# From alternating token tiles to two contiguous token ranges, feature-major, with a list scheduler: a transformer block on eight cores

## The chip, the cores and the metric

One Trainium2 chip, all 8 of its cores. Four pairs of cores take one batch element each. The metric is the device time of the slowest core, in microseconds. A program on all cores has a second, slower state in some executions: the cores of one die show a lower granted clock (0.81 to 0.96 on average where an undisturbed die has 0.96 to 0.98) and the time is 2 to 16% longer.

Engines: PE is TensorE's matmul side and PEld its weight loads, DVE is VectorE, ACT ScalarE, POOL GpSimd, SP the engine that issues the plain DMA queue. GpSimd issues the queue that casts fp32 weights to bf16 on the way.

## The reference

```python
# x: (4, 2048, 2048) fp32; one layer
hn = rms_norm(h, g_pre_mix);  z = hn @ w_in          # [u | q | k | v | f_logit]
y_pool = multiscale_pool(u, w_pool, pool_scale)       # trailing means over 2, 4, 8, 16 frames
y_attn = forgetting_attention(q, k, v, log_sigmoid(f_logit + b_f))   # 8 heads of 128, causal
y = concat(rms_norm(y_pool), rms_norm(y_attn))
h = h + rms_norm(y @ w_out, g_post_mix)
m = square(relu(rms_norm(h, g_pre_mlp) @ w_up)) @ w_down              # 2048 -> 8192 -> 2048
h = h + rms_norm(m, g_post_mlp)
gate = sigmoid(rms_norm(h, g_ple_gate) @ w_gate)
h = h + rms_norm(gate * (p @ w_ple), g_post_ple)
```

## The kernel before

Each core of a pair owns every second tile of 128 tokens (1024 tokens), and all eight run one program. K and V are made for all 2048 tokens on both cores. After the attention the data lie token by feature, so the features that the next matmul contracts over must be brought onto the partitions by transposes on TensorE. Instructions are issued in the order in which Python records them; two streams are interleaved with generators.

```python
def attention(hp, ...):             # the denominator is a 129th column of V
    va = VA[sn][:, tt, hh, 0:129]
    mm(bank(b, 0, 129), pt[:, 0:128], va, first, ...)
    ...
def out_part(i, q):                 # token tile i, 512 output features
    for kc in range(KC):
        mm(bank(b), yT[:, i, kc, :], wout[q][:, kc, :], kc == 0, kc == KC - 1)
    actf(junk(), bank(b), AF.Square, accum=col1(ssq_o, i * 4 + q))   # a sum of squares per row
...
def norm1(i):                       # the statistic is a column: no matmul
    v_sum(col1(s_o, i), ssq_o[:, i * 4:i * 4 + 4])
    rsqrt(col1(r_o, i), col1(s_o, i), float(D))
    v_stt(o, o, col1(r_o, i), xt[i % 2], ALU.mult, ALU.add)
    ...
def transpose_tile(src, gi, dst):   # 16 PE transposes for 128 tokens, then gains on the way out
    pe.op(lambda h: h.transpose(tv[:, k, :], src[:, kc * 128:kc * 128 + 128], ident), ...)
...
def gate(w, q, t):
    ...
    actf(sg, bank(b), AF.Sigmoid, scale=col1(r_3, t))
```

Row sums of squares come out of ScalarE as a by-product (`accum`), and normalising is one VectorE instruction per tile with a per-partition scalar. Hardly anything is asked of GpSimd but DMA issue and 16 copies.

The softmax here doesn't subtract the row's maximum and nothing guards it: scores larger than these inputs give would overflow.

## Time and profile before

| | before |
|---|---|
| time, median of 5 runs | 1696.18 us (1695.76 to 1698.33) |
| TensorE busy | 1590.8 us, 94% |
| VectorE, ScalarE, GpSimd busy | 558.5, 505.1, 121.3 us |
| mean granted clock | 0.98 |
| TensorE work at the prediction's price per matmul | 1560 us |
| the rest: idle and slow-clock time | 136 us |

Every matmul that the trace records is given the prediction's price for its columns; the sum over a core's matmuls, subtracted from the elapsed time of a stage, leaves what the stage lost. The lines of the profile of before that carry the price are in the prediction. (An fp32 matmul is recorded as two, each at the price of a bf16 one. That is too little: at full clock such a record took 203 ns for 240 columns, twice the price. So in the changed kernel some 8 us of "loss" are work, the same 8 in every run below.)

### The profile page before, as it was taken

The page shows a single profiled execution, that of the slowest core. Times are in us where ns is not written, and L with a number is a line of the kernel's source. Part 1 is how long each engine was busy: PE and PEld are TensorE (multiplying, and loading weights), DVE is VectorE, ACT ScalarE, POOL GpSimd, SP SyncE. Part 2 cuts the span into 40 slices and gives each one's busy share as a digit, 9 for nine tenths or more (in the row PEclk, how much of TensorE's full clock was granted, in tenths as well). Part 3 has the DMA queues.
Part 4 walks back from the last instruction along what each step waited for, and adds up shares of the span by engine and source line. Part 5 has one row for each costly group of instructions (what it writes and reads, how often), then busy time and mean ns, then how long its engine had stood idle before and what let it go on. Part 6 is the DMA issues. An engine that isn't in the chain of part 4 may idle for free.

```text
span 1696.4 us, 24256 instructions; the slowest of 8 cores (1691.1 to 1696.4 us)
## 1 busy us (share of the span) xinstructions
PE 1590.8 (94%) x8700; PEld 812.8 (48%) x8700; DVE 558.5 (33%) x915; ACT 505.1 (30%) x1071; POOL 121.3 (7%) x241
## 2 busy tenths in 40 slices
PE   3789999999968999999999999999999999998995
PEld 1447585855544444444444444444444444444442
DVE  3564232322535553112111211121221112475455
ACT  3564544445432543110001100011000111445355
POOL 2012000001000001000101010100101010001000
PEclk9999999999988999999999999999999999999998
DMA  9566223138173549644444353526353546557736
GB/s 241 136 159 93 34 30 46 27 50 125 20 155 50 158 143 190 106 66 84 74 77 78 72 87 63 99 51 100 53 97 62 88 69 134 160 185 188 148 125 223
DMA packets 42308, 175.71 MB, mean 104 GB/s; under 512 B 4688, under 2 KB 4944, under 8 KB 33616
## 3 DMA queue, kind: packets, MB, share of 16 engines
q0 software_dynamic: 31824, 103.20, 37.9%
q1 hardware_dynamic: 10368, 70.96, 12.5%
q8 instruction: 73, 1.20, 0.3%
q14 instruction: 43, 0.35, 0.1%
HBM read 252.16 MB, written 25.17 MB: 163 GB/s over the span
## 4 chain that ended last, share of the span: by engine, by line
PE 84%; DVE 4%; ACT 4%; DMA 4%; issue 3%; DVEq 0%; ACTq 0%; POOL 0%; POOLq 0%; SPq 0%
PE pb L306 83%; DMA wring<-wqkv 1%; DMA grow<-gb 1%; DVE m L339 1%; DVE accd L334 1%; PE pb L687 1%; DVE m L334 1%; ACT sq L324 1%; ACT junkb L324 1%; DMA wring<-wv 1%; ACT h1j L324 1%; DMA pT_sb<-pT 0%; ACT stats L324 0%; ACT VA L324 0%; ACT rstdB L324 0%
## 5 line engine op out<-in xcount | busy, mean ns | idle before, releaser
L306 PE MATMUL pb<-hT,wslot 128*128 128x512 bf16 x2048 | 442.8, 379 | 2.0 <-DVE hT L334 2.0
L306 PE MATMUL pb<-wslot,hidden 128*128 128x512 bf16 x2048 | 443.7, 379 | 0.0
L306 PEld LDWEIGHTS pb<-hT,wslot 128*128 128x128 bf16 x2048 | 200.3, 98 | 243.3 <-issue 2.1
L306 PEld LDWEIGHTS pb<-wslot,hidden 128*128 128x128 bf16 x2048 | 200.1, 98 | 240.3
L324 ACT ACTIVATE rt<-pb 128x512 f32<-128x512 f32 x128 | 76.4, 598 | 691.1 <-PE pb L306 690.6
L334 DVE TENSOR_TENSOR hidden<-rt 128x512 bf16<-128x512 f32 x128 | 88.5, 692 | 352.0 <-ACT rt L324 352.0
L324 ACT ACTIVATE ptb<-pb,biasT 128x256 bf16<-128x256 f32 (+1 forms) x320 | 139.5, 454 | 163.7 <-PE pb L306 162.4
L334 DVE TENSOR_TENSOR m<-m,pb 128x512 f32<-128x512 f32 x96 | 64.8, 686 | 206.5 <-PE pb L306 206.5
L67 POOL DMA_DIRECT2D wslot<-wmlp x128 | 67.9, 548 | 870.1 <-PE pb L306 833.1
L306 PE MATMUL pb<-wslot,hT 128*128 128x512 bf16 x512 | 119.1, 387 | 0.9 <-ACT sgt L324 0.9
L306 PE MATMUL pb<-wo,yT 128*128 128x512 bf16 x512 | 116.7, 385 | 0.0
L306 PE MATMUL pb<-hgo,wring 128*128 128x512 bf16 x384 | 102.9, 389 | 11.9 <-DMA wring<-wqkv 11.9
L306 PE MATMUL pb<-wring,hgo 128*128 128x256 bf16 (+1 forms) x512 | 69.4, 282 | 21.4 <-DMA wring<-wv 15.2
L306 PE MATMUL pb<-VA,ptb 128*128 128x129 bf16 x576 | 82.6, 220 | 4.0 <-ACT ptb L324 3.0
L306 PEld LDWEIGHTS pb<-wslot,hT 128*128 128x128 bf16 x512 | 50.8, 100 | 63.5 <-issue 5.8
L306 PE MATMUL pb<-wring,hgp 128*128 128x256 bf16 (+1 forms) x512 | 70.4, 276 | 11.6 <-DVE hgp L329 11.6
L306 PE MATMUL pb<-QT,KT 128*128 128x256 bf16 (+1 forms) x320 | 79.6, 262 | 0.0
L306 PEld LDWEIGHTS pb<-wo,yT 128*128 128x128 bf16 x512 | 49.9, 99 | 56.6 <-issue 1.7
L306 PEld LDWEIGHTS pb<-VA,ptb 128*128 128x128 bf16 x576 | 53.5, 98 | 34.8 <-issue 9.5
L306 PEld LDWEIGHTS pb<-wring,hgo 128*128 128x128 bf16 x512 | 49.9, 100 | 38.8 <-issue 28.6
L306 PE MATMUL pb<-wu,hgo 128*128 128x512 bf16 x256 | 65.9, 383 | 0.0
L324 ACT ACTIVATE junkb<-m 128x512 bf16<-128x512 f32 x64 | 40.3, 630 | 75.5 <-DVE m L334 74.2
(112 smaller groups left out, 1163.3 us busy)
## 6 DMA issues: line engine op xcount, KB each, us to landing
wslot<-wmlp POOLq DMA_DIRECT2D x128, 512.0 KB, 12.0
xst<-xT SPq DMA_DIRECT2D x16, 1024.0 KB, 6.7
wring<-wqkv POOLq DMA_DIRECT2D x36, 256.0 KB, 8.5
wo<-wout POOLq DMA_DIRECT2D x16, 512.0 KB, 15.3
xt<-xo SPq DMA_DIRECT2D x8, 1024.0 KB, 6.8
h1s<-osb SPq DMA_DIRECT2D x8, 1024.0 KB, 9.1
h1t<-h1s SPq DMA_DIRECT2D x8, 1024.0 KB, 6.7
wslot<-wgate POOLq DMA_DIRECT2D x16, 512.0 KB, 27.5
```

Source lines behind the costliest of these rows:

```text
L67: self.h.dma_start(out=out, in_=in_).then_inc(s[0], 16)
L306: pe.op(lambda h: h.matmul(o, lhsT, rhs, start=bool(start), stop=bool(stop), skip_group_check=True), r=(lhsT, rhs), w=(o,), signal=bool(st ...
L324: act.op(lambda h: h.activation(o, i, func, **kw), r=r, w=w)
L334: (eng or dve).op(lambda h: h.tensor_tensor(o, a, b, op), r=(a, b), w=(o,))
L339: dve.op(lambda h: h.scalar_tensor_tensor(o, a, s, b, op0, op1, accum_out=accum), r=r, w=w)
L687: pe.op(lambda h, k=k, kc=kc: h.transpose(tv[:, k, :], src[:, kc * 128:kc * 128 + 128], ident), r=(src[:, kc * 128:kc * 128 + 128], ident) ...
```

## The change

The intent: fewer columns for TensorE (K and V only where they are needed, no transposes), no waiting between token tiles, and every engine's order decided by a scheduler instead of by hand. Even cores run one program ("arm a") for tokens 0 to 1087, odd cores another ("arm b") for tokens 1088 to 2047, which still needs K and V of all tokens, its own range and the "context" before it. Everything stays feature by token. So a norm's sum over features is a sum over partitions: squares are added up over the 16 feature blocks into one accumulator tile, on VectorE and on GpSimd, and a matmul with a matrix of ones (tile `onesm`) sums and spreads it. The diff replaces nearly the whole file; its core:

```diff
+    def schedule(self, ops):          # list scheduler: earliest start first, then order of recording
+        ...
+                    key = (st, o.idx)
+                    if pick is None or key < pick[0]:
+                        pick = (key, o)
+        ...
+                else:
+                    t = o.end + 0.2   # a result is there 0.2 us after its assumed end
...
-    def transpose_tile(src, gi, dst, r=mmr):
...
-        actf(sg, bank(b), AF.Sigmoid, scale=col1(r_3, t))
+        P.act(s, (pv, 0, w), AF.Exp, scale=-1.0)
+        P.act(s, s, AF.Ln, bias=1.0)
+        P.act(s, s, AF.Exp, scale=-1.0)
...
+    def sumsq(src, acc_, w, firstone, eng, pool=sqo):
+        ...
+            P.act(t[:, 0:w], src, AF.Square)
+            P.tt(acc_[:, 0:w], acc_[:, 0:w], t[:, 0:w], add, eng=eng)
...
+    def out_norm(g):
+        ...
+            P.tt(O4, O4, rBo[:, 0:w].unsqueeze(1).to_broadcast([128, 4, w]), mult)
+            P.tt(O4, O4, X[:, :, 0:w], add, eng="pool" if q == 1 else "dve")
+        ...
+            for k in range(4 * q, 4 * q + 4):
+                sumsq(O[:, k, 0:w], A2, w, k == 0, "pool" if k % 2 else "dve", sqn)
+        ...
+        P.pe([P.mm(pt, onesm, A2[:, 0:w], 0, w, True, True)])
...
+    P.dma("gq", wps, io["wpool"])
...
+    for g in (0, 1):
+        for blk in range(16):
+            down_last(g, blk)          # last quarter of the down projection, token group g
+        scale2(g)
+        norm2(g)                       # recorded ahead of group g + 1
...
+    with nc.If((pid % 2) < 1):
+        arm(True)
+    with nc.Else():
+        arm(False)
```

The accumulators are `aco` (output norms), `n` (norm before the gate) and `acz` (last norm); `m` is the residual in SBUF that the down projection and the gate are evicted into; `st` holds pieces of h1 or h2 read back from HBM; `xs` holds arriving x. A suffix `_a` or `_b` names the arm.

## The prediction

> **What bounds the kernel now.** I read the page's busy table, then the clock and DMA rows of the 40 slices, the chain that ended last, the windows cut at the stage borders, and the instruction groups.
>
> ```profile
> PE 1590.8 (94%) x8700; PEld 812.8 (48%) x8700; DVE 558.5 (33%) x915; ACT 505.1 (30%) x1071; POOL 121.3 (7%) x241
> PE   3789999999968999999999999999999999998995
> ...
> PEclk9999999999988999999999999999999999999998
> DMA  9566223138173549644444353526353546557736
> ...
> PE 84%; DVE 4%; ACT 4%; DMA 4%; issue 3%; DVEq 0%; ACTq 0%; POOL 0%; POOLq 0%; SPq 0%
> ```
>
> TensorE is the bound (84% of the chain), with three weak places: the first three slices, slices 11 to 15, and the last few. The windows and the chain in order of time size them:
>
> ```profile
> 0.00:130.00 130.00, 85.12 (x460) 47.29 (x461) 67.21 (x155) 65.75 (x87) 14.62 (x32) 0.95 0.73 177
> ...
> 400.00:520.00 120.00, 104.04 (x722) 61.27 (x720) 48.69 (x89) 53.85 (x155) 5.02 (x10) 0.91 0.51 95
> 520.00:659.00 139.00, 127.57 (x716) 64.34 (x716) 72.68 (x85) 57.51 (x112) 7.67 (x15) 0.98 0.56 143
> ...
> 1457.00:1550.00 93.00, 83.43 (x466) 40.15 (x463) 62.41 (x57) 48.69 (x95) 7.39 (x14) 1.00 0.59 180
> ...
> 1674.00:1696.40 22.40, 4.31 (x20) 1.76 (x18) 9.73 (x15) 8.11 (x15) 0.00 (x0) 0.67 0.51 189
> ```
> ```profile
> 222.65 86.02 PE pb L306 x671
> ...
> 659.37 797.89 PE pb L306 x3696
> ```
>
> (Window columns: span, busy us and count of PE, weight load, DVE, ACT, POOL, then clock, DMA share, GB/s.) From 659.4 to 1457.3 nothing but TensorE is on the chain: 797.89/3696 = 215.9 ns per 512-column matmul, i.e. columns/2.4 ns plus 2.6 ns. The 86.02 us piece has 671 narrower ones over 200,848 columns: (86,020 - 83,690)/671 = 3.5 ns over. So I price a matmul at columns/2.4 plus 2.6 ns (3.3 ns below 400 columns). Counting the old code's matmuls that way gives, in us, K 111, V 113, Q 55, U 62, attention 65, output projection 111, PE transposes 22, pooling 12, MLP 885, gate 111, PLE 14, statistics 3: **1561**. The other 135 us of 1696 are idle or slow-clock time: startup 129.6 us for 73 us of priced work (56 lost), some 40 around 400-659, some 39 after 1457.
>
> **What the Trainium skill says.**
> - "TensorE: Matmul & The Clock Gate", Part 1: a back-to-back warm matmul costs N/2.4 plus about 2.5 ns. The 215.9 ns agrees.
> - The same part warns of a 13/16 clock once three cores of a die run dense matmuls. This trace doesn't show it: eight cores ran the MLP at 1.00. I take the clock as unchanged.
> - "ScalarE: Activation LUTs", Table sets: a change of function set costs a load of about 2.7 us, and one set holds both exp and ln. The trace has 17 loads of 1.283 us, half the figure; two of these sit in the tail. The change replaces Sigmoid by Exp, Ln, Exp, so nearly all should go.
> - "SBUF — State Buffer", Who interferes with whom: a VectorE instruction with two SBUF inputs and a GpSimd instruction that reads SBUF lock each other out. The old kernel cannot test it: its only GpSimd arithmetic is 16 copies. The new one gives GpSimd hundreds of adds.
>
> ```profile
> L334 DVE TENSOR_TENSOR m<-m,pb 128x512 f32<-128x512 f32 x96 | 64.8, 686 | 206.5 <-PE pb L306 206.5
> L334 DVE TENSOR_TENSOR accd<-accd,sq 128x512 f32<-128x512 f32 x56 | 38.7, 692 | 12.4 <-ACT sq L324 8.1 <-DVE accd L334 1.0
> ...
> L334 DVE TENSOR_TENSOR m<-m,h1t 128x2048 f32<-128x2048 f32 x8 | 18.3, 2293 | 1.4 <-DVE m L339 1.4
> ...
> L324 ACT ACT_TABLE_LOAD x17 | 21.8, 1283 | 9.7 <-DMA xst<-xT 8.4 <-DVE stats L348 0.9
> ```
>
> VectorE on fp32 pairs: (2293 - 692)/1536 = 1.042 ns per column plus 158 ns. ScalarE, from 598 ns at 512 and 1054 at 1024 columns: 0.89 ns per column plus 142.
>
> **The change part by part.** It is a rewrite. Before, each core of a pair takes every second 128-token tile, and all eight run one program with K and V for 2048 tokens. Now an even core runs an arm for tokens 0-1087, with K and V for those alone; an odd core runs an arm for 1088-2047, with K and V for all 2048. Everything stays feature-by-token, so no PE transposes; norm sums become matmuls with a matrix of ones; the attention denominator moves from a 129th V column to a VectorE sum; a list scheduler written into the kernel orders every engine's instructions.
>
> *1. TensorE work, priced as above.* Even arm (us): K, Q, V 182, attention 43, U 59, pooling 7, output 119, up 475, down 475, gate 119, PLE 15, fp32 statistics (four passes per column, as I count them) 15: **1510**. Odd arm: 275, 90, 53, 7, 106, 417, 417, 106, 13, 15: **1498**. Against 1561: saves 51 on the longer arm. The two are within 12 us, so the uneven split 1088/960 looks deliberate.
>
> *2. Startup.* Now 16 chunks of x (8.9 MB), with K and most of Q multiplied as chunks arrive; four weight blocks of 0.52 MB (as bf16) first. Rates from the queue table: the plain queue moved 70.96 MB in 12.5% of 1696 us, 335 GB/s when busy; the casting queue 103.2 MB in 37.9%, 160 GB/s. So 8.9/335 + 2.1/160 = 26.6 + 13.1 = 40 us, plus some 2 us latency and 5 us of statistics, by which V's weights have come: 47 us. TensorE has 22 us of work in it. VectorE per chunk: a scale in two of three (about 0.7 us) and an add of 1088 (1.29), 1.8 us by 16 = 28 us, hidden. Lost: 47 - 22 and some 3 of low clock = **28**, against 56. The old startup, after its first 38 us, was held by square-and-add chains between slabs, not by DMA.
>
> *3. Last attention with pooling.* VectorE, odd arm: 82 denominator adds over 24,448 columns 38.4, masks 4, closings 8; pooling per channel block: evacuation 1.33, window adds 1.75 times 1.17, difference 1.16, scaling 1.32, by 8 = 47. Sum 97 us against 82 of TensorE: 15 lost, plus GpSimd collisions, say **18**. Even arm: 82 against 77: **8**.
>
> *4. Head norms and output projection.* The norm chain (two matmuls, four ScalarE steps, first scaling) about **5**. Output groups: VectorE 23 and GpSimd 9 us per 30 us of TensorE, tight: **4**. The MLP starts on the first two thirds of the tokens, covering the last norm. These replace the old 40 around 400-659.
>
> *5. MLP.* Same bytes per column as before (1.05 MB read per 7.3 us); nothing lost.
>
> *6. From the last down projection.* Norms are hidden per token group behind the next group's matmuls. VectorE adds up to about 190 us of 226, GpSimd 80-100, and many pairs exclude each other: **8**, up to 30 if the lock is strict.
>
> *7. Tail.* The last group has 176 tokens: activations 1.5, sum and statistic 2, 16 scalings at 0.34 and some five adds at 0.52: 8; store 2: **13**, against 18 from the last matmul before.
>
> *8. Branch on the core's number*: **3**, a guess.
>
> Even: 1510 + 28 + 8 + 5 + 4 + 8 + 13 + 3 = 1579. Odd: 1498 + 28 + 18 + 5 + 4 + 8 + 13 + 3 = 1577. Predicted: **1580 us**, 6.8% less. Of the 116 us gain some 51 is less TensorE work, 28 the startup, the rest the middle and the end.
>
> **The rivals.**
> - *VectorE and GpSimd become the bound outside the MLP.* For: steps 3 and 6 are near full before any collision, and a static order can't absorb a late operand. Against: idle VectorE now (33%), and the scheduler was given these durations (its 0.157 + 1.042 per thousand columns is the trace's). It would add 20-50: 1600-1630.
> - *The scheduler fills nearly everything.* For: tens of matmul groups are free to move while one waits. Then only startup, tail and a few gaps remain: 1510 + 40 = 1550.
> - *Transfers.* Pieces of 1.0-1.2 KB per row replace 8 KB rows for x, h1, h2 and the result, and weight loads queue behind GpSimd adds; output weights land where the activations lay, so they wait for the last U matmul. Against: a DMA share of 0.5 now in the MLP. Would add 10-40.
> - *One arm is longer.* The time is the slowest core's; a miscount of one arm goes straight into it, and a gain on the other is worth nothing.
>
> **Range and chances.** The first three rivals span 1550 to 1630; an eight-in-ten range is 1545 to 1628. To miss 2% (1662), losses would have to be 150 us, more than the old kernel's, despite its much worse startup: at or above that I give 8%. Faster by over 2% 0.92, within 0.06, slower 0.02.
>
> **What would show it.** Right: even and odd cores within 20 us of each other, with about 10,900 and 10,100 matmuls; MLP at full clock with no waits; TensorE dense from about 47 us; one or two table loads; no transposes. Wrong: TensorE waiting in the pooling or gate stage on VectorE tiles whose mean time is well above 158 + 1.042 per column (the lock); startup beyond 60 us (DMA slower when two queues share); a gap at the first output block (weights); the two kinds of core 30 us apart; or a clock of 0.8 in the denser stages.

## The result

The changed kernel took **1711.03 us** (median of 7 timed runs, one of them slow; fast ones 1709.49 to 1713.09), against 1695.86 for the kernel before in the same rounds: a ratio of **1.0087** (95% interval 1.0076 to 1.0098). It is 0.9% slower, where 1580 was predicted. (A ratio is the mean time of one kernel's fast runs over the mean of the other's fast runs of the same rounds, so not quite the ratio of the medians quoted.) Executions in which one die ran at a lower clock are left out of the means.

The page of the changed kernel, core 3, an odd one, in the rows that the prediction shows of before (busy time, TensorE and clock and DMA in 40 slices, shares of the chain that ended last):

```profile
PE 1544.3 (90%) x10180; PEld 980.5 (57%) x10180; DVE 786.4 (46%) x1569; ACT 579.2 (34%) x1349; POOL 296.2 (17%) x392
PE   2889999999888887899999999999999999883994
...
PEclk9989999999999998899999999999999999986997
DMA  7951211236009347944544454445444443795056
...
PE 78%; DMA 7%; DVE 7%; issue 4%; ACT 2%; POOL 1%; SPq 1%; DVEq 0%; ACTq 0%; POOLq 0%
```

TensorE's busy time fell by 46 us, VectorE's rose by 228, and the chain runs through DMA and VectorE for 14% where it was 8%. The MLP, slices 18 to 34, is full. The weak places are the first three slices, slices 11 to 17 and, new, slices 35 to 37, after the MLP.

What TensorE waited for (columns: total us, times, longest), core 3:

```profile
PE pb L363 <- DVE m_b L420: 25.4, 3, 12.6
PE pb L363 <- DMA wsl_b<-wk: 19.7, 1, 19.7
PE pb L363 <- DVE n_b L420: 19.2, 3, 16.7
PE pb L363 <- POOL aco_b L420: 18.6, 3, 6.8
```

and core 0, an even one:

```profile
PE pb L363 <- POOL aco_a L420: 39.3, 4, 18.8
PE pb L363 <- DVE n_a L420: 18.0, 3, 11.3
PE pb L363 <- DVE m_a L420: 14.7, 3, 10.5
PE pb L363 <- DMA wsl_a<-wk: 12.5, 1, 12.5
```

Most of these are not waits for data that a large matmul needs. `aco` and `n` are accumulators that feed one small statistics matmul. TensorE takes its instructions in order; where the scheduler put that small matmul a few us before its operand was there, the large ones behind it stood as well. One such place in the timeline (start, us, engine, operation, and in brackets the idle time before):

```profile
559.74 12.77 PE L363 MATMUL pb<-yT_b,wo_b 128*128 128x240 bf16 x123
578.41 1.14 PE L363 MATMUL pb<-aco_b,onesm_b 128*128 128x240 f32 x2 [5.89 <-POOL aco_b L420]
579.34 10.88 PE L363 MATMUL pb<-yT_b,wo_b 128*128 128x240 bf16 x94
```

The output matmuls before and after the gap have nothing to do with `aco_b`, but 5.9 us are gone.

**Where the time went.** My sum over the trace, with the prediction's price for each matmul (us; "before the output" is startup, projections, attention, pooling and head norms up to the first output matmul; the output stage ends with the last statistics matmul of the output norms; "end" runs from the first matmul of the last down projection to the last gate matmul):

| | priced work | before the output | output stage | MLP | end | tail | total |
|---|---|---|---|---|---|---|---|
| odd (core 3), predicted loss | 1498 | 54 | 4 | 0 | 8 | 13 | 1577 |
| odd, found | 1492 | 97.7 | 40.0 | -1 | 61.8 | 21.1 | 1711 |
| even (core 0), predicted loss | 1510 | 44 | 4 | 0 | 8 | 13 | 1579 |
| even, found | 1503 | 77.6 | 48.5 | -2 | 52.6 | 21.3 | 1701 |

("Before the output" is the prediction's startup, pooling, head norms and branch together.) The other cores of a kind lost about the same: in this profile the four odd ones 94.9 to 97.7 us before the output and 61.7 to 62.7 in the end, the four even ones 74.7 to 77.6 and 44.3 to 52.6. In the later runs the spread is up to 10 us (the odd cores' end with the norms mixed in, 26.6 to 35.1), so smaller differences between two runs mean little unless all four cores show them.

The change took 68 us of work from TensorE (1560 to 1492; some 60 with fp32 at its measured cost) and lost 84 us more while TensorE waited or ran below full clock (136 to 220). The question is where those losses come from. Four places: startup (about 69 us in the odd arm by 416 us, 49 in the even arm by 250 us, together with the branch, 31 predicted), the pooling stage with the head norms (some 28.5 in both arms; 23 and 13 predicted), the output stage, and the end.

### The profile page after: what moved, and what is told of

Read it like the earlier page. It is cut to its first block, busy times and chain, and to the rows that moved or that the text cites. A ratio compares the mean times of both kernels' runs of the same rounds, so it can differ in the third digit from the quotient of the medians.

```text
span 1711.5 us, 29071 instructions; the slowest of 8 cores (1688.7 to 1711.5 us)
## 1 busy us (share of the span) xinstructions
PE 1544.3 (90%) x10180; PEld 980.5 (57%) x10180; DVE 786.4 (46%) x1569; ACT 579.2 (34%) x1349; POOL 296.2 (17%) x392
## 3 DMA queue, kind: packets, MB, share of 16 engines
q0 software_dynamic: 28208, 102.77, 35.1%
## 4 chain that ended last, share of the span: by engine, by line
PE 78%; DMA 7%; DVE 7%; issue 4%; ACT 2%; POOL 1%; SPq 1%; DVEq 0%; ACTq 0%; POOLq 0%
PE pb L363 78%; DMA xs_b<-xin 4%; DVE m_b L426 2%; DMA st_b<-h1s 1%; DMA xr_b<-xin 1%; DVE dac_b L420 1%; DVE m_b L420 1%; DVE acc_b L420 1%; DVE aco_b L420 1%; POOL aco_b L420 1%; DVE osb_b L420 1%; SPq L441 0%; ACT ptb_b L393 0%; POOL acz_b L420 0%; ACT sg_b L393 0%
## 5 line engine op out<-in xcount | busy, mean ns | idle before, releaser
L363 PE MATMUL pb<-hT_b,ws_b 128*128 128x480 bf16 (+3 forms) x2560 | 420.0, 327 | 10.5 <-ACT hT_b L393 10.5
L363 PEld LDWEIGHTS pb<-hT_b,ws_b 128*128 128x128 bf16 x2560 | 243.5, 98 | 185.9 <-issue 15.0
L363 PE MATMUL pb<-hid_b,ws_b 128*128 128x480 bf16 x1536 | 311.5, 366 | 0.0
L363 PEld LDWEIGHTS pb<-hid_b,ws_b 128*128 128x128 bf16 x1536 | 150.3, 98 | 160.7
L363 PE MATMUL pb<-hgo_b,wsl_b 128*128 128x512 bf16 (+2 forms) x768 | 188.9, 386 | 37.8 <-DMA wsl_b<-wk 19.7
L393 ACT ACTIVATE ptb_b<-pb,bias_b 128x256 bf16<-128x256 f32 (+3 forms) x328 | 157.8, 508 | 103.9 <-PE pb L363 60.4
L420 DVE TENSOR_TENSOR dac_b<-dac_b,ptb_b 128x256 f32<-128x256 f32 (+3 forms) x304 | 153.4, 508 | 54.8 <-ACT ptb_b L393 43.7
L363 PE MATMUL pb<-hidg_b,ws_b 128*128 128x272 bf16 (+2 forms) x1024 | 109.8, 271 | 15.2 <-DVE m_b L420 15.2
L363 PE MATMUL pb<-h2g_b,ws_b 128*128 128x272 bf16 (+2 forms) x1024 | 116.7, 270 | 3.6 <-ACT sg_b L393 3.0
L363 PE MATMUL pb<-yT_b,wo_b 128*128 128x240 bf16 x1024 | 111.2, 273 | 0.0
L363 PE MATMUL pb<-QT_b,KT_b 128*128 128x256 bf16 (+3 forms) x328 | 82.3, 290 | 1.0 <-ACT ptb_b L393 1.0
```

What stands on the lines that cost most here:

```text
L363: ins = h.matmul(pb[0:rows, pt.bank, lo:hi], lhsT, rhs, start=st, stop=sp_, skip_group_check=True)
L393: return self.rec("act", lambda h: h.activation(of(), if_(), func, **kw), r, [self.key(o)], (0.18 + 0.84e-3 * self.size(i)))
L420: return self.rec(eng, lambda h: h.tensor_tensor(of(), af(), bf(), op), [self.key(a), self.key(b)], [self.key(o)], self.vdur(o, a, b, eng))
```

## The experiments

All edits are to the changed kernel. The theories: **A**, the scheduler plans small statistics matmuls at a moment that the chain of small instructions before them can't keep, and the in-order TensorE stands there; **B**, VectorE and GpSimd lock each other out, so VectorE is late; **C**, transfers are late (x, h1 and h2 in small pieces beside the weights). Losses are given as odd / even, in the table's terms, from cores 3 and 0. All runs gave correct results unless it is said otherwise.

### A: tell the scheduler that statistics come later

```diff
-                    t = o.end + 0.2
+                    t = o.end + 0.2 + q.lag     # 6.0 for the statistics matmuls below, else 0
...
-        P.pe([P.mm(pt, onesm, A2[:, 0:w], 0, w, True, True)])
+        P.pe([P.mm(pt, onesm, A2[:, 0:w], 0, w, True, True)]).lag = LAG   # out_norm; the same in rsq
```

> Edit: only the scheduler's belief changes: the statistics matmuls of the norms (a matrix of ones times a sum of squares) are planned 6 us later than their operand's planned end. Theory A (TensorE's queue is in order, and the plan puts these matmuls before their operand is there; TensorE waits 20 us on the output norm's and some 30 us on the later norms' statistics in the odd arm, 42 and 30 in the even arm): these waits fall by more than half, odd cores 1670 to 1685 us, even cores 1650 to 1670. Theory B (VectorE and GpSimd as a pair are too slow in these stages, whatever the order): TensorE waits as long, only at other matmuls; within 10 us of 1711.

Measured: 1690.0 us (one fast run; before 1695.2 to 1697.1), mean spans 25 us less on the odd cores and 36 us less on the even ones. Output stage 40.0 / 48.5 to **20.4 / 10.2**; end 61.8 / 52.6 to 58.9 / 49.6. (The odd cores stayed just above the 1670 to 1685 expected.) No work was removed: every engine runs the same instructions as before. Their order is planned anew, though, on TensorE and, less intended, on the others too. In the output stage, 530 to 720 us, TensorE's waits in the kernel with the lag are

```profile
PE pb L365 <- ACT hT_b L395: 9.7, 2, 6.0
PE pb L365 <- DMA ws_b<-wup: 1.3, 1, 1.3
PE pb L365 <- DVE aco_b L422: 1.3, 1, 1.3
```

The wait on `aco_b`, 18.6 us, is down to 1.8 (0.5 of it for an addition on GpSimd, not shown). So theory A holds for the output stage. What the plan had wrong, the 0.2 us between engines or the durations that it assumes, this run does not separate: 6 us cover both. In the end the waits for `n_b` vanished too, but those for `m_b` grew from 25.4 to 42.2 us: there something else is late.

### B: no arithmetic on GpSimd

```diff
     def tt(self, o, a, b, op, eng="dve"):
+        eng = "dve"
```

> Edit: every GpSimd tensor addition goes to VectorE; the plan is made again. Theory B (lock between a VectorE instruction with two SBUF inputs and a GpSimd addition, and sums that pass from one engine to the other): VectorE's scalings of m drop from 719 ns to about 441 (158 + 1.042 x 272), the broadcast multiply of 960 columns from 1661 to 1158; the output and end stages lose 20 to 50 us less, the pooling stage 10 to 20 us more; in all 1670 to 1705. If the lock costs nothing: VectorE durations stay, VectorE has some 95 us more to do, 1730 to 1760.

Measured: 1704.9 us (one fast run). Output stage 49.0 / 52.3, no better; end **39.3 / 32.6**, 20 us better. The 10 to 20 us more that were expected of the pooling stage were not there: with the head norms it lost some 6 and 2 us more. Groups with two SBUF inputs on VectorE, changed kernel (busy us, then the mean in ns, ahead of the last bar), with the GpSimd adds among them:

```profile
L420 DVE TENSOR_TENSOR osb_b<-osb_b,rBo_b 128x960 f32<-128x960 f32 x16 | 26.2, 1661 | 4.0 <-ACT rBo_b L393 4.0
L420 POOL TENSOR_TENSOR aco_b<-aco_b,sqn_b 128x240 f32<-128x240 f32 x32 | 31.6, 988 | 30.9 <-DVE aco_b L420 22.5 <-ACT sqn_b L393 5.2 <-ACT sqo_b L393 2.4
L426 DVE SCALAR_TENSOR_TENSOR m_b<-m_b,cst_b,n_b 128x272 f32<-128x272 f32 x32 | 21.5, 719 | 0.2 <-ACT n_b L393 0.2
```

and the same work without GpSimd:

```profile
L421 DVE TENSOR_TENSOR osb_b<-osb_b,rBo_b 128x960 f32<-128x960 f32 x16 | 18.1, 1153 | 3.7 <-ACT rBo_b L393 3.7
L421 DVE TENSOR_TENSOR aco_b<-aco_b,sqn_b 128x240 f32<-128x240 f32 x60 | 24.3, 405 | 2.0 <-ACT sqn_b L393 1.2 <-DVE aco_b L421 0.5 <-ACT rt_b L393 0.2
L427 DVE SCALAR_TENSOR_TENSOR m_b<-m_b,cst_b,n_b 128x272 f32<-128x272 f32 x32 | 15.1, 496 | 0.3 <-ACT n_b L393 0.3
```

The same instructions take 1153 ns and not 1661, 496 and not 719. The first of the shorter figures is at the prediction's 158 ns + 1.042 ns per column (1158), the second, which also multiplies by a gain, 55 ns over it (441). The lock is real, and the longer means hide how it works. Of the sixteen 960-column multiplications in the changed kernel twelve took 1144 to 1159 ns, and four 3182 to 3193. Each of the four began while a GpSimd addition was running, here the first of them (start, us):

```profile
559.34 2.95 POOL L420 TENSOR_TENSOR osb_b<-osb_b,xr_b 128x960 f32<-128x960 f32 x1 [14.08 <-DVE osb_b L420]
560.11 3.19 DVE L420 TENSOR_TENSOR osb_b<-osb_b,rBo_b 128x960 f32<-128x960 f32 x1
```

The addition ends at 562.29, VectorE's instruction at 563.30, so it waited out the addition and did the rest, 1.01 us, after it. Evictions that take one operand from PSUM were not held up: `m_b<-m_b,pb` of 272 columns took 430 ns on the mean beside GpSimd and 434 alone.

Yet in the output stage TensorE still waits for `aco_b`, now made by VectorE alone, 31.5 us: removing the lock is no cure there, and run A, which kept GpSimd's adds, shows that the order is.

### C: first MLP weights and gate weights after the reads that they meet

```diff
-    bload(blocks[len(phys) - 1])
+    bload(blocks[len(phys) - 1], after=[xr_op[0]])     # after the last read of x
...
-        bload(("gt", 0, blk))
+        bload(("gt", 0, blk), after=[st_op[0]])        # after the second group's last read of h1
```

> Edit: the MLP's first weight blocks (all but two) are issued only after the last load of x for the output norm, and the gate's weights only after the last load of h1 of the second token group. Theory C (small loads stand behind a flood of weights: 18.5 us for x at 667, 19.1 us for h1 at 1483 in the odd arm): both long waits fall under 6 us, odd cores 1685 to 1700. Theory A or B: the waits become waits for weights or for VectorE, within 8 us of 1711.

Measured: 1717.6 and 1714.6 us, ratio to before 1.0116 (1.0087 to 1.0146), so no gain. Output stage 48.4 / 48.4, end 54.3 / 61.0. The edit did what it was meant to: the last two pieces of x landed in 6.1 and 7.2 us at most (odd, even), where they had taken 19.0 and 26.6. But the waits for `aco` did not shrink (38.0 and 39.3 us). As the bound of the output stage, theory C falls. For the end this run only shows that holding the gate weights back gains nothing; a later run shows why.

### The branch: test for odd cores first

```diff
-    with nc.If((pid % 2) < 1):
-        arm(True)
-    with nc.Else():
-        arm(False)
+    with nc.If(((pid + 1) % 2) < 1):
+        arm(False)
+    with nc.Else():
+        arm(True)
```

> Edit: the branch tests for odd cores first, so that the odd arm's code comes first and the even arm is the far side of the branch. Theory D (the far side starts 6 us later: first x load at 9.6 us in the odd arm, 3.3 in the even one): the starts change places, odd cores 1703 to 1707 us, even cores 1703 to 1708; the time 1703 to 1708. If transfers hide the late start: odd cores stay at 1709 to 1711.

Measured: 1712.0 and 1708.9 us. The odd cores are 8 us sooner (mean span 1710.4 to 1702.3), the even ones 7 us later (1696.7 to 1704.2). So the far side of the branch costs some 7 us; in the changed kernel the odd arm's first load of x is issued at 9.6 us and the even arm's at 3.3. Turning it moves the cost to the other arm.

### A and B together, first try

The lag as above, and the GpSimd adds after the MLP's last down projection (not those before the MLP) on VectorE:

```diff
-        sumsq(md, acm[g], w, blk == 0, "pool" if blk % 2 else "dve", sqm)
+        sumsq(md, acm[g], w, blk == 0, "dve", sqm)      # the same at the four other places of the end
```

> Both changes at once: the scheduler is told that the statistics matmuls of the output and later norms come 6 us later, and the GpSimd adds after the MLP's last down projection (not those before the MLP) go to VectorE. The lag alone freed the output stage (odd arm's loss 40 to 20 us, even arm's 48 to 10) and left the end at 59 and 50; the end with every add on VectorE and no lag lost 39 and 33. Theory (two independent causes, an order planned too tight in the output stage and the lock in the end): odd output loss near 20 and end loss near 39 or below, time near 1670, even cores near 1640. Rival (the end is held by VectorE's sheer work, the lock only a part of it): the lag and the moved adds overlap, end loss stays above 50 in the odd arm, time stays at 1685-1690.

Measured: 1683.45 us, ratio 0.9908 (0.9851 to 0.9965). Output stage 18.7 / 12.1, but the end 57.0 / 54.8: the 20 us that the lockless end had won were not there. The first theory, of two causes that simply add, failed here. What differs from the run without GpSimd is the lag on the statistics *after* the MLP. New theory: that lag itself costs the end as much as the lock, since there the next matmuls hang on the norm.

### The lag on the output norms alone

```diff
-        P.pe([P.mm(pt, onesm, acc_[:, 0:w], 0, w, True, True)]).lag = LAG      # rsq
+        P.pe([P.mm(pt, onesm, acc_[:, 0:w], 0, w, True, True)])
```

> As the run with the lag and the moved adds, but the lag is on the statistics matmul of the output norms alone, not on those after the MLP. Theory (the lag itself cost the end what the moved adds had won: it put the later norms 6 us later): output loss near 19 (odd) and 12 (even), end loss near 39 (odd) and 33 (even) as in the run with all adds on VectorE; odd cores near 1665. Rival (the moved adds did not free the end; the gain seen there belonged to the whole order of that kernel): end loss stays above 50.

Measured: 1671.9 and 1668.3 us, ratio 0.9829 (0.9806 to 0.9853). Output 19.5 / 9.8, end **38.6 / 38.3** (39 and 33 expected). As the new theory had it: the lag helps where other matmuls are free to move up, and costs where they are not. What remains in the end (from 1340 us on) is one kind of wait:

```profile
PE pb L365 <- DVE m_b L422: 31.0, 6, 16.0
PE pb L365 <- DVE acz_b L422: 2.9, 1, 2.9
```

`m_b` is written both by a norm and by the eviction of the next group's down projection. The scheduler prefers what was recorded first, and a whole norm (some 40 VectorE instructions) was recorded ahead of the next group. So evictions, which free TensorE's accumulators, queue behind it. That is theory D.

### D: norms mixed into the next group, GpSimd kept and not

```diff
+def mix(*parts):                       # interleave by count of instructions
+    ...
-        scale2(g)
-        norm2(g)
+    norm2(0); N = P.take()
+    for blk in range(16):
+        down_last(1, blk)
+    scale2(1); T = P.take()
+    L.extend(mix((N, 0, 0.8), (T, 0, 1)))       # the same for groups 2, 3 and for the gates
```

With GpSimd's adds kept in the end:

> Lag on the output norms as in the last run; GpSimd keeps its adds; and after the MLP each norm's instructions are recorded mixed, by count, among the next group's matmuls and their evictions, where the change records them as a block ahead. The scheduler prefers what was recorded first, so VectorE did some 40 instructions of a norm before the evictions that free TensorE's accumulators. Theory D (TensorE stands in the end because its evictions queue behind a norm on VectorE): end loss from 62 and 53 to 35 or less. Rival (the lock's longer VectorE times are the cause): end loss stays above 50, since VectorE's work and the lock are as before.

With them on VectorE:

> Both: the mixed order and the adds of the end on VectorE, with the lag on the output norms. If order and lock are independent causes, the end loss falls below both of the last two runs, to about 15-25; if they are one cause seen twice (VectorE late, whatever for), it is close to the lower of the two. Output loss 19 and 12. Odd cores 1640-1665.

Measured: 1672.0 us in both runs with GpSimd's adds, 1659.4 and 1659.9 without (ratios 0.9841 and 0.9768, the latter 0.9747 to 0.9789). The loss of the end, odd / even, all with the lag on the output norms alone except the first, which is the changed kernel itself:

| | norm ahead of the next group | norm mixed in |
|---|---|---|
| GpSimd adds in the end | 61.8 / 52.6 | 43.4 / 41.9 |
| VectorE alone in the end | 38.6 / 38.3 | 32.0 / 28.5 |

Neither expectation was met as written (35 or less against above 50; 15 to 25 against the lower of the two). Either cure gives 11 to 23 us, both give 24 to 30 (on the mean of the four cores of a kind, the cells are 62 / 49 and 42 / 42, 40 / 39 and 32 / 29, so 8 to 22 and 20 to 30). I read them as two ways for VectorE to be late for the same evictions, which is why they add only in part.

### Startup: the bytes

The pooling weights have no buffer to wait for, so they are loaded amid x, and in the even arm the first output and MLP weights wait for them and follow:

```diff
-    P.dma("gq", wps, io["wpool"])
+    P.dma("gq", wps, io["wpool"], after=[xdma[-1]])
```

> The pooling weights, and with them the first output weights that wait for them, are loaded after the last load of x and not in the middle of it. Theory (the startup is bound by the bytes that the DMA engines must move before the last chunk of x has come): 1.0 to 1.5 MB of cast weights leave the first 50 us of the even arm; at 160 GB/s of the casting queue that is some 6 us of DMA time shared with x, so the loss up to 80 us falls from 44 to about 38 in the even arm; in the odd arm 0.5 MB leave and the loss up to 130 us falls from 64 to about 61. Rival (the startup is bound by latency of each chunk's chain, load, scale, matmul): no change of more than 1 us. The time itself: 1705 to 1711.

Measured: 1710.5 and 1708.0 us. The loss up to 80 us in the even arm 43.6 to **37.7**, up to 130 us in the odd arm 64.2 to **58.8**; mean spans 8 us less (even) and 6 us less (odd).

The other test leaves out the second range of x, in the odd arm alone:

```diff
-        xdma.append(P.dma("sp", X, io["xin"][kc, :, a:b], after=after))
+        if first or b > 1024:           # the context keeps what the buffers hold
+            xdma.append(P.dma("sp", X, io["xin"][kc, :, a:b], after=after))
```

> Wrong result on purpose: the odd arm does not load x for its context range (8.4 MB) but works on what its staging buffers hold; the even arm is as it was. Theory (the odd arm's startup waits for the sheer bytes of both ranges of x): the gaps after 60 us go, that is 25 of the odd arm's 64 us of loss up to 130 us; some 40 us of loss remain, those before 60 us. Rival (the waits after 60 us are on weights and on the order of the instructions): the loss up to 130 us stays above 58. Odd cores would end 10 to 25 us sooner under the theory, the even cores at about 1697 set the time.

Measured: 1701.3 us, the odd cores 16 us sooner on the mean. The result passed the comparison although the context is stale. (The first odd query lies 65 tokens past the last stale one and b_f is about 3, which lets a key fade by some 5% a step; that explanation was not tested.) Windows of the changed kernel and of this one (span, busy us and count of PE, PEld, DVE, ACT, POOL, then clock, DMA share, GB/s):

```profile
0.00:60.00 60.00, 26.65 (x101) 10.17 (x102) 22.44 (x29) 21.65 (x21) 4.08 (x11) 1.00 0.79 198
60.00:130.00 70.00, 56.26 (x300) 32.05 (x299) 39.55 (x56) 29.47 (x37) 3.23 (x6) 0.90 0.73 172
```
```profile
60.00:130.00 70.00, 67.28 (x450) 44.93 (x451) 37.96 (x56) 26.48 (x38) 2.08 (x4) 1.00 0.30 48
```

Without the second range's 8.4 MB TensorE is busy for 67 of 70 us and not 56, and the loss up to 130 us is 43.8, not 64.2. Core 3 is the best of the four odd ones: together they lost 43.8 to 53.2, against 61.8 to 64.2, so 15 us less on the mean. So the odd arm's startup lost 15 to 20 us to the second range of x, 5 to weights that were not needed yet and some 7 to the branch. The rest, up to 60 us, I put down to the time that the first range takes to come in (its last piece landed at 62.5 us); no run tests that.

### Pooling: VectorE without the denominators

```diff
+                    if p == 3:
+                        if j == 0:
+                            P.set(da[:, 0:w], 1.0)
-                    if j == 0:
+                    elif j == 0:
                         P.cp(da[:, 0:w], pt[:, 0:w])
                     else:
                         P.tt(da[0:rows, c0:w], da[0:rows, c0:w], pt[0:rows, c0:w], add)
```

> Wrong result on purpose: the last attention, which runs beside the pooling, has no sums of its denominators (82 VectorE adds and 6 copies, 38 us in the odd arm, become 6 fills). The pooling stage lost about 26 us in both arms. Theory (VectorE is the bound of this stage, as the prediction's step 3 has it): the loss of this stage falls to under 10 us. Rival (the loss comes from the GpSimd adds in the window sums, or from the order): it falls by less than 8. The time follows with 1690 to 1700 under the theory.

Measured: 1698.2 us in the one fast run (wrong result). The stage in the changed kernel and without the denominators:

```profile
420.00:440.00 20.00, 18.91 (x107) 9.58 (x106) 18.91 (x40) 11.85 (x25) 2.88 (x2) 1.00 0.04 7
440.00:520.00 80.00, 65.39 (x340) 32.05 (x338) 74.37 (x124) 41.16 (x87) 32.08 (x30) 0.98 0.11 22
```
```profile
420.00:440.00 20.00, 20.00 (x115) 10.69 (x114) 16.30 (x24) 15.13 (x34) 5.59 (x5) 1.00 0.01 1
440.00:520.00 80.00, 74.76 (x472) 48.23 (x470) 58.06 (x106) 39.70 (x96) 33.59 (x32) 0.96 0.44 83
```

VectorE was busy for 93 of 100 us and TensorE for 84; with 19 us taken from VectorE in this stretch TensorE is busy for 95. The odd arm's loss from 416 to 490 us goes from 15 to 1 us; some 8 remain where the head norms follow. So VectorE is the bound of this stage in the odd arm, and the loss of the whole stage falls under 10 us as expected. In the even arm it does not: there the stage goes from 28.8 to 18.3 us (18.1 to 18.3 on all four cores), more than the rival allowed and less than the theory asked, so VectorE's denominators are a part of that loss and the rest is open.

### All that helped, and what was left of the end

Lag on the output norms, end on VectorE, norms mixed in, late pooling weights, odd arm tested first:

> All that helped so far: lag on the output norms, adds of the end on VectorE, mixed order, pooling weights after x, and the test of the core's number turned so that the odd arm starts first. From the run before, odd cores should gain 5 (late weights) and 6 (start), even cores gain 6 and lose 6: the time near 1640 to 1650, that is 0.970 of the kernel before. If the losses only move from stage to stage, it stays above 1665.

Measured: 1659.0 us (median; fast 1658.1 to 1659.1), ratio **0.9764 (0.9743 to 0.9785)**: 2.4% faster than the kernel before. Odd losses: 78.8 before the output, 18.6, end 34.0, tail 24.0. But 1640 to 1650 had been expected, and the even cores, mean 1653, became the slower ones. With 34 / 30 us still lost in the end, three more runs were made. First, the gate weights held back again (the edit of the transfer run, its second half):

> The last kernel, with the gate weights held back until the second token group's h1 has been read. Theory (the loads of h1 are slow because gate weights share the DMA engines, and VectorE stands up to 10 us for one of them): end loss from 34 and 30 to about 25 and 22. Rival (the gate weights are then themselves late, or the wait moves to VectorE's own work): end loss 30 or more, time 1655 or above.

Measured: 1675.2 and 1668.6 us. The end lost 42.5 / 49.9, so the rival's figure. But the windows show what happened, here the kernel with everything and then with held-back weights:

```profile
1420.00:1500.00 80.00, 64.63 (x634) 56.36 (x632) 55.76 (x152) 27.61 (x80) 8.99 (x17) 0.91 0.93 178
1500.00:1520.00 20.00, 17.03 (x141) 13.05 (x140) 19.44 (x49) 15.34 (x44) 0.00 (x0) 1.00 0.60 175
```
```profile
1420.00:1500.00 80.00, 76.24 (x763) 67.22 (x761) 66.47 (x179) 35.93 (x103) 8.98 (x17) 1.00 0.78 153
1500.00:1520.00 20.00, 1.38 (x9) 0.53 (x7) 2.65 (x7) 1.75 (x5) 0.00 (x0) 0.57 1.03 208
```

and the DMA view of 1425 to 1475 us (size, then median us from issue to landing), in the same order:

```profile
ws_b<-wgate POOLq DMA_DIRECT2D x12, 512.0 KB, 10.7
...
st_b<-h1s SPq DMA_DIRECT2D x4, 272.0 KB, 24.0
```
```profile
st_b<-h1s SPq DMA_DIRECT2D x4, 272.0 KB, 5.7
...
st_b<-h1s SPq DMA_DIRECT2D x4, 256.0 KB, 26.9
```

Held back, the second group's pieces of h1 land in 5.7 us and not 24, and TensorE is busy for 76 of 80 us and not 65. Then the third group's pieces meet the same weights, land in 26.9 us, and 19 of the next 20 us are lost. The clash is real; the edit only moves it to a later group. (In the even arm the small load of p also queued behind the weights, and TensorE stood 34.5 us for it.)

Second, without most of the reads:

```diff
-            P.dma("sp", H, io["h1s"][:, 2 * q:2 * q + 2, a:b], r=...)
+            if g == 0 and q < 4:
+                P.dma("sp", H, io["h1s"][:, 2 * q:2 * q + 2, a:b], r=...)
```

> Wrong result on purpose: the last kernel, but the norms after the MLP load only four of their 32 pieces of h1 and reuse them. Theory (transfers hold the rest of the end): end loss falls by 12 or more in both arms, to about 20. Rival (VectorE's own work holds it): falls by less than 6.

Measured (wrong result): 1643.7 us in the fast run. End 34.0 / 30.5 to **17.3 / 22.1**. The odd arm meets the transfer theory, the even arm's 8 us lie between the two.

Third, the branch as it was:

> The last kernel, but with the even arm tested first again. If the far side of the branch costs about 6 to 8 us wherever it is: odd cores near 1654, even cores near 1645, so about 5 us less or the same as the last kernel's 1659, ratio to the kernel before 0.974 to 0.978.

Measured: one fast run of four, 1652.4 us, against 1696.7 to 1697.7 for the kernel before on this chip: 0.974, without an interval. Mean spans 1635 (even) and 1650 (odd), to be set against 1653 and 1647 with the branch turned. Turning it won the odd arm 4 us and cost the even arm 18. The two runs were on different chips, but that is not the reason: the two runs before this one, with the branch turned and on this very chip, lost the even arm as much before the output and in the output stage (82.3 and 20, 79.0 and 19) as the turned kernel on the other chip (82.9 and 19), where this run lost 71.0 and 12. Some 12 of the 18 us fall in the startup (the wait for the first K weights is 23.3 us and not 11.8), where the odd arm in turn won 12.8; some 7 are in the output stage, and why is open. The odd arm's losses later, up to 4 us a stage, gave most of its gain back.

| kernel (odd / even loss, us) | before the output | output | end | tail |
|---|---|---|---|---|
| the change | 97.7 / 77.6 | 40.0 / 48.5 | 61.8 / 52.6 | 21.1 / 21.3 |
| lag everywhere | 99.5 / 75.0 | 20.4 / 10.2 | 58.9 / 49.6 | 19.4 / 22.6 |
| no GpSimd arithmetic | 101.4 / 79.1 | 49.0 / 52.3 | 39.3 / 32.6 | 20.8 / 23.8 |
| lag on output norms, end on VectorE | 96.8 / 72.6 | 19.5 / 9.8 | 38.6 / 38.3 | 20.2 / 25.3 |
| the same, norms mixed in | 91.4 / 77.3 | 19.8 / 12.5 | 32.0 / 28.5 | 21.2 / 24.6 |
| the same, pooling weights late | 91.6 / 71.0 | 17.5 / 12.3 | 30.7 / 29.0 | 20.3 / 23.6 |

## Why the prediction was wrong

*Step 1, TensorE work: right.* 1492 and 1503 us found in the trace (some 1500 and 1511 with fp32 at its measured cost), 1498 and 1510 predicted (10,180 and 11,025 matmuls, some 10,100 and 10,900 predicted). The two arms are within 12 us of each other in work, and no transposes are left.

*Step 5, the MLP: right.* From 700 to 1400 us TensorE is busy throughout at clock 1.00.

*The small expectations: right.* One table load per arm, of 1283 ns. Even and odd cores within 20 us: about 1697 and 1710, though both arms missed their predicted time by as much, some 120 and 130 us. (Slips in the working that moved nothing: the rounded prices of the old matmuls add up to 1564, not 1561, where the trace gives 1560; three table loads, not two, lie after 1674 us; ScalarE's line is drawn through one instruction that reads PSUM and one that reads SBUF.)

*Step 2, startup: mis-sized, about 69 and 49 us with the branch in place of 28 + 3.* The rates taken from before were nearly right: with the pooling weights delayed, the even arm's x came in within 42 us (3.1 to 45.5), where 40 were reckoned. The volume was not. I counted the even arm's x and four weight blocks, 11 MB. In the first 130 us core 3 moved 23.96 MB, because the odd arm loads a second range of x at once (15 to 20 us, shown by leaving it out) and pooling weights come early (5 to 6 us, shown by delaying them). One arm's count was applied to both. That leaves some 12 us or more of the miss in each arm that no run accounts for; V's weights, reckoned to be there at 47 us, landed at 55 to 70 in the even arm.

*Step 8, the branch: 3 guessed, some 7 found*, on the odd arm, and 12 of startup once the pooling weights were out of the way.

*Step 3, pooling: mechanism right for the odd arm, size off for the even arm.* In the odd arm VectorE is the bound, as the step had it. With the head norms of step 4 the stage lost some 28.5 in both arms, where 23 and 13 were predicted; in the even arm 18 of them stayed when VectorE's denominators went.

*Step 4, output groups: the step that failed outright, 4 predicted, 40.0 and 48.5 found.* It compared busy times (23 us of VectorE per 30 of TensorE) and took whatever fits for hidden. It did not ask in which order TensorE meets the statistics matmul. An order fixed beforehand with an assumed 0.2 us between engines put it ahead of its operand, and an in-order engine can't step around it. Reordering alone gave back 20 and 38 us. The prediction has the sentence "a static order can't absorb a late operand", but in the rival's list, priced with the lock; without GpSimd's adds the waits are all there.

*Step 6, the end: 8 predicted, "up to 30 if the lock is strict", 61.8 and 52.6 found.* The same way of reckoning missed three things: evictions behind whole norms on VectorE (mixing them in: -18 / -11), the lock (-23 / -14), together -30 / -24, and single reads of h1 that took 24 us beside the gate weights and held VectorE's queue (leaving them out took another 17 / 8). Again an average was used, 190 of 226 us of VectorE, and an average can't show that the 190 stand in the wrong order.

*Step 7, the tail: 21 found, 13 predicted*, in both arms. No run was aimed at it; without GpSimd's adds it was 20.8 and 23.8.

*The rivals.* The first, VectorE and GpSimd as a bound outside the MLP, was true and too small at 20 to 50 us. The third, transfers at 10 to 40 us, was true for the startup and the end and false for the output stage. Each was priced as if the others were absent; added up, even at their own figures, they reach 1580 + 50 + 40 = 1670, beyond the range's upper end of 1628. The range took them one at a time. And 150 us of losses were given 8% as being "more than the old kernel's, despite its much worse startup": a comparison with the very startup figure that was wrong. The losses came to 220 and 198 us.

What stays open: the tail, some 12 us or more of each arm's startup, 18 us of the even arm's pooling stage, the last 10 us or so of the output stage's odd arm (waits for `hT_b`, 9.7 us), the remaining 17 and 22 us in the end, and why turning the branch cost the even arm 7 us as late as the output stage.

## What to carry to other kernels

Busy shares say what can be hidden, not what is; for a static order, go through each in-order queue and ask of every small instruction that depends on a long chain (a norm's statistic above all) what stands behind it if it is late, and record evictions ahead of work that nothing waits for. Moving adds to GpSimd slows the VectorE instructions with two SBUF inputs beside them, so it pays only where VectorE is not what the matmuls wait for. When a change swaps work for overlap, price each stage's losses with all rivals at once, and count the startup's bytes for each program that differs.

## What the Trainium skill lacked or had wrong

- "SBUF — State Buffer", Who interferes with whom: right, the two-input rule shows here: a VectorE multiplication that met a GpSimd addition waited for its end (3.19 us and not 1.15). What it lacks is a size for mixed streams: with 193 GpSimd additions in core 3's program, VectorE's pairs rose on the mean from 496 to 719 ns (272 columns) and from 1153 to 1661 ns (960 columns), that is by about 45%.
- "DMA: Bandwidth & Descriptors", Anatomy of one DMA, fits a lone transfer issued by GpSimd with 2.0 us plus its bytes at 436 GB/s, under 3 us for 0.27 MB. No page says how long a plain transfer takes while weight casts share the engines: 24.0 and 26.9 us here, 5.7 when those were held back.
- "TensorE: Matmul & The Clock Gate", Part 1, expects 13/16 of the clock once three cores of a die run dense matmuls. In the fast runs eight cores ran the MLP at 1.00; only in slow runs did a die average less, 0.81 to 0.96 over the run. The page doesn't tell which state a run will be in.
- "ScalarE: Activation LUTs", What ACT_TABLE_LOAD costs, splits its 2.7 us for a change of set into 1283 ns of load and some 1380 ns of drain. Both kernels' traces have the load at 1283 ns (so the prediction's "half the figure" compared a part with the whole), but no drain: in the trace of before, 14 of the 17 loads stand between two ScalarE instructions that are 1.31 us apart.
- "Runtime: NRT & Kernel Launch", Instruction fetch mechanics, says that a taken branch to a far target has to wait for its instructions, but no page gives a size: on the far side of the branch on the core's number the first load of x was issued at 9.6 us and not 3.3. That this is the fetch was not tested.
- No page warns that a TensorE queue with small matmuls planned too early stalls the large ones behind them: up to 39.3 us for four such waits here.
